# The weights' rings at one end of SBUF and the layers' tiles at the other

## The chip, the cores and the metric

One core of one Trainium2 chip runs the whole program. The metric is the device time of one execution in microseconds (us), as the median over several runs. A difference of about 0.2% (2 us) is what a measurement of this kernel can tell from none.

## The reference, cut to what matters

Three transformer layers work on 256 tokens of width 1024, in float32. Each has a mixer and a gated feed-forward block of inner width 2816:

```python
h = rms_norm(x, norm_mix_g[layer])
x = x + mixer(h, ...)                          # layer 0: sparse attention and pooling
h = rms_norm(x, norm_ffn_g[layer])             # layer 1: stick-breaking attention
x = x + (silu(h @ w1) * (h @ w3)) @ w2         # layer 2: retention and block attention, gated
```

Nearly all the arithmetic is products of the 256 tokens with weight matrices that are read once, 172.6 MB in all.

## The kernel before, in words

A float32 product is made of three float32r products: each operand is split into a high part (hi) and a rest (lo), and hi x hi, hi x lo and lo x hi are added up (`mm3`, L198 to L204; lo x lo is dropped). The stationary operand of a matmul is 128 x 128 of the transposed tokens, the moving operand 128 x 512 of a weight matrix. Each matmul has its own weight load (LDWEIGHTS), which runs while the matmul before it streams.

**The weights** come through `Stream` (L112 to L168). SP loads 1 MB at a time into one of 4 slots w_raw (8 KiB a partition each); ScalarE copies a piece of 1024 words to w_hi (L147), VectorE subtracts to get w_lo (L148); both have rings of 5 slots of 4 KiB a partition. `tick` (L296) keeps the loads and splits ahead of the matmuls.

**proj** (L315 to L347) makes 512 columns of a product over 8 blocks k of the width: for each piece (two k) six matmuls for the first 128 tokens into one accumulator, then six for the second 128 into another. Its stationaries are xT_hi and xT_lo, the normalized tokens. **outproj** (L353 to L397) makes all 1024 columns at once in four accumulators (128 tokens x 512 columns each): for each k and each half of the tokens it issues six matmuls at L368, on the two accumulators in turn. The last four k (the tail; two in the stick layer) are done accumulator by accumulator, 12 matmuls on each. Its stationaries are the layers' own tiles: hT_hi and hT_lo in the three feed-forward blocks (264 x 3 matmuls), mixT in the sparse layer, qT (reused for the attention's result) in the stick layer, moT, A0 and A1, B and C in the second layer.

Attention, transposes and norms are generators that `tick` steps between the matmuls. Line 832 in the stick layer multiplies parts of the constants cst_r (stationary) with sk_sh and sk_sl (moving, 384 columns); lines 1039 to 1041 in the retention multiply ret_sh and ret_sl (stationary) with A (moving, 256 columns).

**Where tiles lie.** Pools opened in `__init__` (L171 to L186) stay open to the end; each layer opens pools of its own and closes them, and the next layer's take the same bytes. All are laid from the low end of a partition's SBUF upwards in the order of opening. Bytes in a partition:

| tiles | before |
|---|---|
| const pool: ident, gains, cst_r (17,280) and others | 16,512 to 21,384 |
| w_raw | 21,408 to 54,176 |
| w_hi, w_lo | 54,176 to 74,656, 74,656 to 95,136 |
| x | 95,136 to 103,328 |
| xT_hi, xT_lo | 103,328 to 111,520, 111,520 to 119,712 |
| junk and the small pool | 119,712 to 124,448 |
| layers' pools | 124,448 to at most 222,752 |
| of these hT_hi, hT_lo | 124,448 to 146,976 to 169,504 |
| mixT | 173,632 to 190,016 |
| qT in the stick layer | 124,448 to 140,832 |
| sk_sh, sk_sl | from 197,152 |
| moT, B, C, A0 and A1 | 124,448, 132,640, 140,832, 157,216 to 181,792 |
| ret_sh | from 216,608 |

Counted modulo 512, the slots of w_hi and w_lo and xT_hi and xT_lo all start at 416; hT, the stick layer's qT, moT, A, B, C, sk_sh and ret_sh at 32; mixT at 64; the part of cst_r that L832 loads at 384. Steps inside a tile, from one stationary to the next or one moving piece to the next, are multiples of 512 bytes here.

Of the kernel before, what the change touches and what calls it, by code (L numbers as in the profile page):

```python
# [37 lines left out]
AHEAD = 4  # L38
# [73 lines left out]
class Stream:  # L112


    def __init__(self, nc, raw, hi, lo, ahead_load, ahead_split):
        self.nc, self.raw_p, self.hi_p, self.lo_p = nc, raw, hi, lo
        self.al, self.asp = ahead_load, ahead_split
        self.slots, self.pieces = [], []
        self.raws, self.parts = {}, {}
        self.i = self.loaded = self.split = 0  # L120
# [50 lines left out]
class Kernel:  # L171
    def __init__(self, ctx, tc, a, out):
        self.tc, self.nc, self.a, self.out = tc, tc.nc, a, out
        pool = lambda name, bufs, **kw: ctx.enter_context(tc.tile_pool(name=name, bufs=bufs, **kw))
        self.cp = pool("const", 1)
        self.raw = pool("raw", 4)
        self.hi = pool("whi", AHEAD + 1)
        self.lo = pool("wlo", AHEAD + 1)
        self.act = pool("act", 1)
        self.small = pool("small", 4)  # L180
        self.acc = pool("acc", 4, space=bass.MemoryType.PSUM)
        self.z = pool("z", 2, space=bass.MemoryType.PSUM)
        self.misc = pool("misc", 2, space=bass.MemoryType.PSUM)
        self.now = self.seq = 0
        self.late = slice(P, T)
        self.tasks = []  # L186
# [968 lines left out]
```

## Time and profile before

| what | value |
|---|---|
| median of 3 runs | 1026.62 us (1026.05 to 1026.72) |
| the profiled execution | 1026.29 us |
| its span, first to last instruction | 1024.2 us |
| TensorE (PE) busy | 1007.5 us, 4790 matmuls |
| weight loads (PEld) busy | 827.8 us |
| VectorE (DVE) busy | 631.1 us |
| ScalarE (ACT) busy | 548.5 us |
| HBM read | 172.60 MB, 170 GB/s over the span |

PE is the matmuls, PEld the weight loads, SPq SyncE's DMA queue. Matmuls are pipelined: one is recorded for longer than the distance to the next, so busy time doesn't tell how fast TensorE goes. The distance from one matmul's start to the next one's does. In the view of the chain in order of time, a piece "x220" is 220 matmuls one behind the other, with the time that they took together.

### The profile page before, as it was taken

What the parts mean: (1) busy time and instruction counts of PE and PEld (TensorE: products, weight loads), DVE (VectorE), ACT (ScalarE), POOL (GpSimd) and SP (SyncE); (2) the same over time, 40 slices, a digit from 0 to 9 for tenths busy, and PEclk for the clock granted to TensorE, in tenths of its full rate; (3) what the DMA queues carried; (4) which work ended last, traced back from release to release, by engine and by line L of the source; (5) the groups of instructions that cost most, each with busy time, mean ns of one, the idle gap of its engine ahead of it and who ended that gap; (6) DMA issues with size and microseconds to landing.
All of it is one profiled execution on the core that took longest, in us unless ns stands there. A gap on an engine that the chain in (4) does not pass through costs nothing.

```text
span 1024.2 us, 12484 instructions
## 1 busy us (share of the span) xinstructions
PE 1007.5 (98%) x4790; PEld 827.8 (81%) x4790; DVE 631.1 (62%) x896; ACT 548.5 (54%) x822; POOL 71.2 (7%) x171
## 2 busy tenths in 40 slices
PE   7999999999999999999999999999999999999998
PEld 6777888888778888788888888888887888888886
DVE  5987655554466888655554467666777665555542
ACT  7566544443467776744444366675444464444431
POOL 2321000000040000200000024000020010000000
PEclk9999999999999999999999999999999999999999
DMA  9443655555555333455555546455535546555531
GB/s 329 166 154 106 218 174 185 185 188 182 165 173 197 98 109 124 132 197 187 183 192 178 187 143 205 135 185 187 183 124 173 187 137 233 174 199 174 193 135 41
DMA packets 80747, 174.45 MB, mean 170 GB/s; under 512 B 3120, under 2 KB 16048, under 8 KB 80688
## 3 DMA queue, kind: packets, MB, share of 16 engines
q1 hardware_dynamic: 80400, 173.57, 49.8%
q8 instruction: 37, 0.61, 0.2%
q14 instruction: 22, 0.18, 0.0%
q10 hardware_dynamic: 288, 0.09, 0.0%
HBM read 172.60 MB, written 1.05 MB: 170 GB/s over the span
## 4 chain that ended last, share of the span: by engine, by line
PE 90%; DVE 4%; POOL 2%; ACT 2%; issue 1%; DMA 1%; SPq 0%; DVEq 0%; ACTq 0%
PE acc L368 27%; PE acc L202 18%; PE acc L204 18%; PE acc L203 18%; PE misc L223 4%; DVE w_lo L148 1%; POOL is_y L232 1%; PE z L204 1%; PE misc L202 1%; PE misc L203 1%; PE z L202 1%; PE misc L204 1%; PE z L203 1%; DMA x<-in_x_dram 1%; DVE sc L729 0%
## 5 line engine op out<-in xcount | busy, mean ns | idle before, releaser
L148 DVE TENSOR_TENSOR w_lo<-w_raw,w_hi 128x1024 fp32r<-128x1024 f32 (+1 forms) x323 | 392.9, 1222 | 298.4 <-ACT w_hi L147 298.1
L147 ACT CAST w_hi<-w_raw 128x1024 fp32r<-128x1024 f32 (+1 forms) x323 | 337.4, 1050 | 350.9 <-PE acc L204 225.9
L202 PE MATMUL acc<-w_hi,xT_hi 128*128 128x512 f32 (+2 forms) x896 | 352.8, 394 | 0.0
L204 PE MATMUL acc<-w_hi,xT_lo 128*128 128x512 f32 (+2 forms) x896 | 347.7, 388 | 0.0
L203 PE MATMUL acc<-w_lo,xT_hi 128*128 128x512 f32 (+2 forms) x896 | 347.7, 388 | 0.0
L204 PEld LDWEIGHTS acc<-w_hi,xT_lo 128*128 128x128 f32 x896 | 168.9, 188 | 34.8
L202 PEld LDWEIGHTS acc<-w_hi,xT_hi 128*128 128x128 f32 x896 | 169.0, 189 | 32.2 <-ACT xT_hi L213 1.0
L203 PEld LDWEIGHTS acc<-w_lo,xT_hi 128*128 128x128 f32 x896 | 169.2, 189 | 31.3
L368 PE MATMUL acc<-w_hi,hT_hi 128*128 128x512 f32 x264 | 105.1, 398 | 0.0
L368 PE MATMUL acc<-w_lo,hT_hi 128*128 128x512 f32 x264 | 104.1, 394 | 0.0
L368 PE MATMUL acc<-w_hi,hT_lo 128*128 128x512 f32 x264 | 86.9, 395 | 0.0
L368 PEld LDWEIGHTS acc<-w_hi,hT_hi 128*128 128x128 f32 x264 | 49.6, 188 | 12.5
L368 PEld LDWEIGHTS acc<-w_hi,hT_lo 128*128 128x128 f32 x264 | 49.6, 188 | 11.7
L368 PEld LDWEIGHTS acc<-w_lo,hT_hi 128*128 128x128 f32 x264 | 49.6, 188 | 10.9
L267 POOL TENSOR_TENSOR norm_s<-norm_ss 128x1 f32<-128x1 f32 x12 | 3.4, 282 | 597.6 <-ACT junk L263 597.6
L214 DVE SCALAR_TENSOR_TENSOR xT_lo<-misc,gains,xT_hi 128x128 fp32r<-128x128 f32 (+1 forms) x84 | 28.0, 353 | 21.1 <-ACT xT_hi L213 21.0
L213 ACT ACTIVATE xT_hi<-misc,gains 128x128 fp32r<-128x128 f32 (+1 forms) x84 | 29.0, 370 | 11.4 <-DVE xT_lo L214 9.5
L441 ACT ACTIVATE sg<-acc,norm_rstd 128x512 f32<-128x512 f32 (+1 forms) x36 | 23.6, 655 | 17.7 <-PE acc L204 17.0
L402 DVE TENSOR_TENSOR x<-acc,x 128x512 f32<-128x512 f32 x24 | 16.6, 690 | 14.2 <-PE acc L368 13.7
L446 DVE SCALAR_TENSOR_TENSOR hid<-acc,norm_rstd,sg 128x512 f32<-128x512 f32 (+1 forms) x36 | 23.9, 700 | 1.6 <-ACT sg L441 1.6
L263 ACT ACTIVATE junk<-x 128x512 f32<-128x512 f32 x24 | 15.2, 632 | 16.6 <-DVE x L402 14.7
L232 POOL TENSOR_TENSOR is_y<-is_v,mhalf 128x1 f32<-128x1 f32 (+2 forms) x24 | 23.8, 992 | 2.0
(265 smaller groups left out, 985.0 us busy)
## 6 DMA issues: line engine op xcount, KB each, us to landing
w_raw<-in_ffn_w_dram SPq DMA_DIRECT2D x62, 1024.0 KB, 5.0
w_raw<-in_w_in_dram SPq DMA_DIRECT2D x26, 1024.0 KB, 4.9
w_raw<-in_w_ffn_down_dram SPq DMA_DIRECT2D x11, 1024.0 KB, 5.0
w_raw<-in_w_ffn_gate_dram SPq DMA_DIRECT2D x10, 1024.0 KB, 5.0
w_raw<-in_w_ffn_up_dram SPq DMA_DIRECT2D x10, 1024.0 KB, 5.0
w_raw<-in_od_w_qkv_dram SPq DMA_DIRECT2D x8, 1024.0 KB, 5.1
w_raw<-in_ev_w_in_dram SPq DMA_DIRECT2D x5, 1024.0 KB, 6.5
w_raw<-in_ev_w_out_dram SPq DMA_DIRECT2D x4, 1024.0 KB, 6.4
```

The lines of the kernel that those rows point to most:

```text
L147: nc.scalar.copy(hi, raw)
L148: nc.vector.tensor_sub(lo, raw, hi.bitcast(F32))
L202: nc.tensor.matmul(out, ah, bh, start=start, stop=False, skip_group_check=True)
L203: nc.tensor.matmul(out, ah, bl, start=False, stop=False, skip_group_check=True)
L204: nc.tensor.matmul(out, al, bh, start=False, stop=stop, skip_group_check=True)
L213: nc.scalar.mul(hi, src, scale)
L214: nc.vector.scalar_tensor_tensor(lo, src, scale, hi.bitcast(F32), op0=OP.mult, op1=OP.subtract)
L223: self.nc.tensor.transpose(out, in_, self.ident)
L232: nc.gpsimd.tensor_tensor(y, v, self.mhalf[:, :width], op=OP.pow)
L368: mm = lambda a, b, start, stop: self.nc.tensor.matmul(o, a, b, start=start, stop=stop, skip_group_check=True)
L441: nc.scalar.activation(s[:, :m], acc[:, :m], AF.Silu, scale=n["rstd"][:, h:h + 1])
L446: nc.vector.scalar_tensor_tensor(t[:, :m], acc[:, :m], n["rstd"][:, h:h + 1], sg[h][:, :m], op0=OP.mult, op1=OP.mult)
```

## The change

The three pools of the weights' rings are opened on the right side: they are laid from the high end of SBUF downwards, and so end at byte 229,344, from 155,616 on. Everything opened after them on the left side (x, xT, the small pool, the layers' pools) moves down by the size of the rings, 73,728 bytes, which is a multiple of 512: x starts at 21,408, xT_hi at 29,600, the layers' pools at 50,720. The const pool stays. Modulo 512 the rings start at 480 and all others where they did.

```diff
         self.cp = pool("const", 1)
-        self.raw = pool("raw", 4)
-        self.hi = pool("whi", AHEAD + 1)
-        self.lo = pool("wlo", AHEAD + 1)
+
+        self.raw = pool("raw", 4, side="right")
+        self.hi = pool("whi", AHEAD + 1, side="right")
+        self.lo = pool("wlo", AHEAD + 1, side="right")
         self.act = pool("act", 1)
```

## Rows read from the trace of the kernel before

**Rows 1.** The page, busy time by engine, and the granted clock in 40 slices

```profile
PE 1007.5 (98%) x4790; PEld 827.8 (81%) x4790; DVE 631.1 (62%) x896; ACT 548.5 (54%) x822; POOL 71.2 (7%) x171
...
PEclk9999999999999999999999999999999999999999
```

**Rows 2.** The page, the chain that ended last, by engine and by line

```profile
PE 90%; DVE 4%; POOL 2%; ACT 2%; issue 1%; DMA 1%; SPq 0%; DVEq 0%; ACTq 0%
PE acc L368 27%; PE acc L202 18%; PE acc L204 18%; PE acc L203 18%; PE misc L223 4%; DVE w_lo L148 1%; POOL is_y L232 1%; PE z L204 1%; PE misc L202 1%; PE misc L203 1%; PE z L202 1%; PE misc L204 1%; PE z L203 1%; DMA x<-in_x_dram 1%; DVE sc L729 0%
```

**Rows 3.** Who waited for whom, and SP's queue: us in total, times, longest

```profile
ACT w_hi L147 <- PE acc L204: 225.9, 153, 3.8
...
PEld misc L223 <- DMA x<-in_x_dram: 6.0, 3, 4.1
...
SPq L136 <- DVE w_lo L148: 751.9, 135, 17.8
```

**Rows 4.** Timeline, proj, ten matmuls: start us, us, engine, line, tiles

```profile
139.74 0.39 PE L202 MATMUL acc<-w_hi,xT_hi 128*128 128x512 f32 x1
...
141.78 0.39 PE L202 MATMUL acc<-w_hi,xT_hi 128*128 128x512 f32 x1
```

**Rows 5.** The chain in order of time, pieces of outproj: start us, us

```profile
225.28 51.34 PE acc L368 x220
...
961.50 58.81 PE acc L368 x252
```

**Rows 6.** Windows: us, busy of PE, PEld, DVE, ACT, POOL; clock, DMA share, GB/s

```profile
127.00:144.00 17.00, 17.00 (x76) 14.08 (x76) 9.49 (x10) 7.59 (x8) 0.00 (x0) 1.00 0.55 178
...
1010.00:1019.00 9.00, 9.00 (x41) 7.22 (x40) 2.08 (x3) 0.00 (x0) 0.00 (x0) 1.00 0.16 58
```

**Rows 7.** Timeline, the last outproj's tail, nine matmuls

```profile
1009.40 0.40 PE L368 MATMUL acc<-w_hi,hT_lo 128*128 128x512 f32 x1
...
1011.27 0.40 PE L368 MATMUL acc<-w_lo,hT_hi 128*128 128x512 f32 x1
```

**Rows 8.** Timeline, proj after an interruption by transposes

```profile
37.50 0.39 PE L204 MATMUL acc<-w_hi,xT_lo 128*128 128x512 f32 x1
...
38.66 0.39 PE L203 MATMUL acc<-w_lo,xT_hi 128*128 128x512 f32 x1
...
39.79 0.39 PE L202 MATMUL acc<-w_hi,xT_hi 128*128 128x512 f32 x1
```

**Rows 9.** Groups by line and shape: busy us, mean ns, idle before

```profile
L148 DVE TENSOR_TENSOR w_lo<-w_raw,w_hi 128x1024 fp32r<-128x1024 f32 x320 | 389.7, 1224 | 296.9 <-ACT w_hi L147 296.5
L202 PE MATMUL acc<-w_hi,xT_hi 128*128 128x512 f32 x864 | 342.5, 396 | 0.0
```

**Rows 10.** Window over the whole span, line 368 alone: PE, PEld

```profile
0.00:1024.20 1024.20, 297.56 (x1224) 226.48 (x1224) 1.00 0.50 170
```

**Rows 11.** Timeline, the stick layer's line 832 and what follows

```profile
350.98 0.34 PE L832 MATMUL z<-sk_sh,cst_r 128*128 128x384 f32 x1
351.15 0.34 PE L832 MATMUL z<-sk_sl,cst_r 128*128 128x384 f32 x1
351.33 0.22 PE L834 MATMUL z<-sk_sh,cst_r 128*128 128x128 f32 x1
```

**Rows 12.** Timeline, 256 columns: ten matmuls of proj, six of the retention

```profile
27.05 0.28 PE L202 MATMUL acc<-w_hi,xT_hi 128*128 128x256 f32 x1
...
28.13 0.28 PE L202 MATMUL acc<-w_hi,xT_hi 128*128 128x256 f32 x1
...
753.15 0.28 PE L202 MATMUL misc<-A,ret_sh 128*128 128x256 f32 x1
...
753.75 0.28 PE L204 MATMUL misc<-A,ret_sl 128*128 128x256 f32 x1
```

**Rows 13.** Weight loads by line and shape: busy us, mean ns

```profile
L203 PEld LDWEIGHTS acc<-w_lo,xT_hi 128*128 128x128 f32 x896 | 169.2, 189 | 31.3
...
L202 PEld LDWEIGHTS misc<-A,ret_sh 128*128 128x128 f32 x12 | 2.3, 190 | 0.8 <-issue 0.7
```

## The prediction

> **What bounds the kernel now.** First the page's busy times and slices: TensorE is busy for 1007.5 us of the span of 1024.2 [rows 10], and the granted clock is full, 2.4 GHz, all the way [rows 1]. The profiled execution took 1026.29 us, 2.1 more than its span; the median of the runs is 1026.62, so sums against this execution come out 0.3 low. Second the chain that ended last: 90% of it is TensorE, over 80% the matmuls of proj (L202 to L204) and outproj (L368) on the accumulators [rows 2]. Third the waits: the copy that makes w_hi waits for TensorE to give ring tiles back (225.9 us behind proj's alone), and SP's loads wait 751.9 us for w_lo's maker to give raw slots back, so the stream of weights runs ahead; of TensorE's own waits the longest is 6.0 us, for x at the start [rows 3]. So the time is the number of matmuls times the gap from the start of one to the start of the next, and the gap is what to look at.
>
> There are two gaps for one shape (128x128 stationary, 512 columns, float32r). In proj nine gaps take 2.04 us: 226.7 ns each [rows 4]. In outproj the chain has 220 matmuls in 51.34 us and 252 in 58.81: 233.4 ns each [rows 5]. The granted clock is 1.00 in both [rows 6]. The slow gap is still there after 1010 us, where ScalarE does nothing, VectorE runs three instructions and the DMAs are at 0.16 [rows 6, 7], so it isn't other engines or loads that make it. After an interruption proj too is slow at first: the five gaps from 37.50 to 38.66 make 232 ns each, the next five, to 39.79, 226 [rows 8]. I call these the fast and the slow rhythm.
>
> **What the change does, part by part.** It issues no instruction more or less, moves none, adds no wait: pools are opened in the same order, so the layers' pools reuse each other's bytes as before, each 73,728 bytes lower. Only bytes change. Matmuls between two of the layers' tiles keep their distances. Four things could feel the rest.
>
> DMAs into w_raw: 170 GB/s on average, a busy share of 0.50, with the loads waiting for free slots [rows 3, 10]. Any small change is hidden by slots loaded ahead: 0 us.
>
> The splits: w_lo's subtraction, the longer of the two, takes 1,224 ns 320 times, 389.7 us in all and 296.9 idle before it, beside 1,007 of TensorE [rows 9]. It would have to slow by a factor before the rings of five ran dry; 0 us. What is not under TensorE on the chain (VectorE 4%, POOL 2%, ScalarE 2%, DMA 1%: some 92 us [rows 2]) I bound at 1% either way, 0.9 us, since no row shows such an instruction changing with the place of its tiles; I take 0.
>
> Outproj: 1,224 matmuls [rows 10]. All their stationaries (mixT, hT, qT, moT, A, B, C) lie at byte 124,448 or above; all of proj's (xT) end at 119,712. After the change every stationary of outproj ends below 116,300, so if height is what separates the rhythms, all 1,224 fall to 226.7. That is 6.7 x 1,224 = 8.2 us at most; the 192 of mixT and qT stand between pieces of attention, and after an interruption even xT's are slow for five gaps [rows 8], so I count them half: 6.7 x (1,032 + 96) = 7.5 us. The other end is 0; that they get slower still no steady row suggests, and the rivals' prices cover it.
>
> Proj: 864 x 3 = 2,592 matmuls of 512 columns [rows 9]. Below, kept rhythm: 0. Above, all of them in the slow rhythm: 6.7 x 2,592 = 17.4 us; some 288 of them (stick layer, six projections of 48) stand between attention's matmuls and mostly never settle, so 15.4. I take 0, for this reason. Byte distance is the second thing that separates the rhythms: counted modulo 512, xT starts 0 bytes from the ring tile that streams meanwhile, hT, qT, moT, A, B and C 128, mixT 160. After the change these are 448 (xT), 64 and 96 (mixT). The trace has one more distance: in the stick layer L832 loads parts of cst_r 352 bytes from the tile that streams, and its gaps are 170 and 180 ns for 384 columns [rows 11]. What should it be? Proj with 256 columns stands 120 ns apart and with 512 226.7, so a column costs 0.417 ns and a matmul 13.3 more [rows 4, 12]; 384 columns then make 173 in the fast rhythm, 180 in the slow. A mean of 175 is near the fast one. So 0 and 352 are fast or nearly, 128 and 160 slow; 448 lies between 352 and 512, which is 0 again, and I expect proj to stay fast. For outproj 64 lies halfway from fast to slow: by this reading the gain is about half, 3.8 us.
>
> Is it height or distance? The stationaries of L202 to L204 on ret_sh, at byte 216,608 and distance 0 from A, which streams, stand 120 ns apart at 256 columns, just as proj's at 256 columns do [rows 12]. That speaks against height. Weight loads take 189 ns from xT and 190 from ret_sh [rows 13], which speaks against it too. The distance would do, but rests on four values. Both readings give a gain, so the sum is **1026.3 - 7.5 = 1018.8; against the median 1019**, with 1022.8 for the half gain.
>
> The Trainium skill, "TensorE: Matmul & The Clock Gate", in "Step-by-step: what each phase is for", says that TensorE has two read ports of SBUF of its own, so that loading the next weights takes no bandwidth from the running matmul. By that rule no tile's place could change a gap and the sum would be 1026.3. The trace has two gaps for one shape [rows 4, 5], which the rule doesn't explain; the ports themselves no row shows.
>
> **The rivals.**
> *Same: the order of work makes the slow rhythm.* Outproj alternates two accumulators and takes a new ring tile for each k; proj stays on one accumulator and uses a tile for two k. Then nothing moves: 1026.3. Against it: in outproj's tail twelve matmuls run on one accumulator, as in proj, and are no faster (1009.40 to 1011.27: eight gaps, 234 ns) [rows 7]. For it: nothing else rules it out, and the two gaps may also hang on bytes that keep their distance to each other. This is also how the change would do nothing of what it says: 0.24.
>
> *Slower: proj loses its rhythm.* If distance 0 is a special case and any other gives the slow rhythm, 448 is slow too. Place: all proj's stretches; price 15.4 us: 1041.7. For it: the only steady fast gaps in the trace have distance 0 [rows 4, 12]; after interruptions proj itself runs at the slow gaps [rows 8], as if slow were the rule. Against it: L832. It decides as soon as proj loses more than 7.5 us / 2,592 = 2.9 ns a matmul. 0.25. With outproj at 64 fast all the same, 1034.2: 0.10.
>
> *Much faster: the matmul's fixed part goes.* 13.3 ns in proj, 20 in outproj: 2,592 x 13.3 + 1,224 x 20 = 59 us, 967. Against it: pairs of tiles at most 60 KB apart (proj) and 180 KB apart (L832) both show it [rows 4, 11]. 0.02.
>
> **How the numbers follow.** Outproj fast and proj fast, 1017 to 1021: 0.28. Half gain, around 1022.8: 0.11. Much faster 0.02. That is 0.41 for faster by over 0.2% (2 us, about what a measurement of this kernel can tell from no change); 0.24 for within; 0.25 + 0.10 = 0.35 for slower. Signs are mixed, so the likeliest case's own range is 1017 to 1021, and the range of all reaches from 1017 to 1042: it leaves out the much faster case, the upper half of the 15.4 us case and some of the edges, under 0.2.
>
> **What would show it.** Right: in the chain, outproj's long pieces at about 226.7 ns a matmul (220 in 49.9 us instead of 51.34), proj's nine gaps still 2.04 us, all counts of instructions unchanged, TensorE's clock at 1.00, the busy times of ScalarE and VectorE as now. Half right: outproj's pieces near 230. Wrong, same: 51.34 us again. Wrong, slower: nine gaps of proj at 2.10 us and the span at 1039. I would be wholly wrong if the instructions stood in another order, or if a wait for w_lo showed on TensorE.

## The result and the profile after

| | before | after |
|---|---|---|
| median of 5 runs | 1026.62 us (1026.05 to 1028.32) | 1031.82 us (1030.82 to 1034.97) |
| span of the profiled execution | 1024.2 us | 1029.7 us |
| TensorE busy, matmuls | 1007.5 us, 4790 | 1013.5 us, 4790 |

The ratio after to before is 1.0051, 95% interval 1.0036 to 1.0066: the changed kernel is **slower** by about half a per cent, where the forecast was 0.7% faster. In the changed kernel all line numbers from 176 on are higher by one: L202 to L204 are L203 to L205, L368 is L369.

The page of the kernel after (busy time and number of instructions by engine; the granted clock in 40 slices; the chain that ended last, by engine), against [rows 1, 2]:

```profile
PE 1013.5 (98%) x4790; PEld 829.0 (81%) x4790; DVE 631.0 (61%) x896; ACT 548.3 (53%) x822; POOL 71.3 (7%) x171
...
PEclk9999999999999999999999999999999999999999
...
PE 90%; DVE 4%; POOL 3%; issue 2%; ACT 1%; DMA 1%; SPq 0%; DVEq 0%; ACTq 0%; POOLq 0%
```

The same instructions, and VectorE, ScalarE and GpSimd as busy as they were; TensorE takes 6.0 us more. (A slice of the clock is 26 us long and its digit 9 says 90% or more, so the short dip told below doesn't show in it.) The splits and the loads didn't change either. The group of w_lo's subtraction by shape, against [rows 9]:

```profile
L148 DVE TENSOR_TENSOR w_lo<-w_raw,w_hi 128x1024 fp32r<-128x1024 f32 x320 | 389.5, 1223 | 302.2 <-ACT w_hi L147 301.7
```

And the waits of SP's queue and of the copies to w_hi (us in total, times, longest), against [rows 3]:

```profile
ACT w_hi L147 <- PE acc L205: 229.7, 153, 3.9
...
SPq L136 <- DVE w_lo L148: 757.6, 135, 17.8
```

One subtraction takes 1223 ns (1224 before), and the loads still wait over 750 us for free slots. So the stream is as far ahead as it was, and the place to look at is again the gap between matmuls.

**Outproj is unchanged.** The chain in order of time, the long pieces of outproj (start us, us), against [rows 5]:

```profile
225.90 51.36 PE acc L369 x220
...
547.75 51.36 PE acc L369 x220
...
966.99 58.84 PE acc L369 x252
```

51.36 and 58.84 us, where before had 51.34 and 58.81: 233.4 ns a matmul, the slow gap. None of the 7.5 us came.

**Proj is slower.** For this I take a longer stretch than [rows 4]: 72 gaps in one unbroken run of proj in the last feed-forward block. The timeline of before, the first and the last of its 73 matmuls:

```profile
841.48 0.39 PE L204 MATMUL acc<-w_hi,xT_lo 128*128 128x512 f32 x1
...
857.80 0.40 PE L204 MATMUL acc<-w_hi,xT_lo 128*128 128x512 f32 x1
```

And the timeline of after, the same 73 matmuls:

```profile
846.07 0.39 PE L205 MATMUL acc<-w_hi,xT_lo 128*128 128x512 f32 x1
...
862.55 0.40 PE L205 MATMUL acc<-w_hi,xT_lo 128*128 128x512 f32 x1
```

16.32 us before, 16.48 after: 226.67 against 228.89 ns a matmul. Over the three matmuls of one float32 product (hi x hi, hi x lo, lo x hi) that is 680.0 against 686.7 ns, so each triple has lost 6.67 ns, 16 steps of the 2.4 GHz clock. All 24 long runs of proj in the trace of after (more than 30 matmuls without a break) settle at this figure within 0.2 ns; I call it the settled gap. Proj has 864 triples, which would make 5.8 us if all were in such runs; matmul for matmul the two traces drift apart by 4.3 us from 30 us on, the dip told next left out, and 4.2 of them lie in proj. It is less than 5.8 since the gaps right after an interruption were slow before too [rows 8].

The spans differ by 5.5 us. The rest is one step of 1.6 us at the border of the first two layers, and a start that is 0.4 us shorter. Windows of after and then of before (us, busy of PE, PEld, DVE, ACT, POOL, granted clock, DMA share, GB/s):

```profile
286.00:299.00 13.00, 10.80 (x52) 8.61 (x51) 8.24 (x15) 8.91 (x18) 9.89 (x12) 1.00 0.59 206
299.00:302.40 3.40, 3.40 (x10) 2.62 (x9) 2.63 (x3) 1.53 (x3) 0.00 (x0) 0.50 0.41 142
```

```profile
286.00:299.00 13.00, 10.74 (x52) 8.63 (x51) 8.33 (x15) 8.63 (x19) 9.52 (x12) 1.00 0.67 228
299.00:302.40 3.40, 3.40 (x16) 2.77 (x16) 2.68 (x4) 2.23 (x3) 0.00 (x0) 1.00 0.26 73
```

In the profiled execution of after TensorE was granted half its clock (1.2 GHz) for 3.4 us: 10 matmuls instead of 16. Ahead of it the engine had stood idle for 2.2 us in 13, as long as in before, whose clock stayed at 1.00. Such a dip is in the profiled executions of six of the ten kernels below (faster ones and slower ones) and missing in the others. What decides it is open; I count it as 1.6 us that the execution had and that no run here puts down to a place of tiles.

### The profile page after: what moved, and what is told of

Its sections match the earlier page's. It is cut to its first block, busy times and chain, and to the rows that moved or that the text cites. A ratio compares the mean times of both kernels' runs of the same rounds, so it can differ in the third digit from the quotient of the medians.

```text
span 1029.7 us, 12484 instructions
## 1 busy us (share of the span) xinstructions
PE 1013.5 (98%) x4790; PEld 829.0 (81%) x4790; DVE 631.0 (61%) x896; ACT 548.3 (53%) x822; POOL 71.3 (7%) x171
## 4 chain that ended last, share of the span: by engine, by line
PE 90%; DVE 4%; POOL 3%; issue 2%; ACT 1%; DMA 1%; SPq 0%; DVEq 0%; ACTq 0%; POOLq 0%
PE acc L369 27%; PE acc L203 18%; PE acc L205 18%; PE acc L204 18%; PE misc L224 4%; POOL is_y L233 1%; PE z L205 1%; PE z L203 1%; DVE w_lo L148 1%; PE misc L204 1%; PE misc L203 1%; PE z L204 1%; PE misc L205 1%; POOL kT L880 1%; DMA x<-in_x_dram 1%
## 5 line engine op out<-in xcount | busy, mean ns | idle before, releaser
L203 PE MATMUL acc<-w_hi,xT_hi 128*128 128x512 f32 (+2 forms) x896 | 356.0, 398 | 0.0
L205 PE MATMUL acc<-w_hi,xT_lo 128*128 128x512 f32 (+2 forms) x896 | 349.8, 391 | 0.0
L204 PE MATMUL acc<-w_lo,xT_hi 128*128 128x512 f32 (+2 forms) x896 | 348.6, 389 | 0.0
L205 PEld LDWEIGHTS acc<-w_hi,xT_lo 128*128 128x128 f32 x896 | 169.2, 189 | 37.6
L204 PEld LDWEIGHTS acc<-w_lo,xT_hi 128*128 128x128 f32 x896 | 169.5, 189 | 32.8
L203 PEld LDWEIGHTS acc<-w_hi,xT_hi 128*128 128x128 f32 x896 | 169.4, 189 | 32.1 <-ACT xT_hi L214 0.9
L369 PE MATMUL acc<-w_hi,hT_hi 128*128 128x512 f32 x264 | 105.2, 398 | 0.0
L369 PE MATMUL acc<-w_lo,hT_hi 128*128 128x512 f32 x264 | 104.4, 396 | 0.0
L369 PE MATMUL acc<-w_hi,hT_lo 128*128 128x512 f32 x264 | 86.9, 395 | 0.0
L369 PEld LDWEIGHTS acc<-w_hi,hT_hi 128*128 128x128 f32 x264 | 49.6, 188 | 12.3
L369 PEld LDWEIGHTS acc<-w_hi,hT_lo 128*128 128x128 f32 x264 | 49.6, 188 | 11.8
L369 PEld LDWEIGHTS acc<-w_lo,hT_hi 128*128 128x128 f32 x264 | 49.6, 188 | 11.1
L214 ACT ACTIVATE xT_hi<-misc,gains 128x128 fp32r<-128x128 f32 (+1 forms) x84 | 29.2, 369 | 11.4 <-DVE xT_lo L215 9.1
```

Source lines behind the costliest of these rows:

```text
L203: nc.tensor.matmul(out, ah, bh, start=start, stop=False, skip_group_check=True)
L204: nc.tensor.matmul(out, ah, bl, start=False, stop=False, skip_group_check=True)
L205: nc.tensor.matmul(out, al, bh, start=False, stop=stop, skip_group_check=True)
L214: nc.scalar.mul(hi, src, scale)
L369: mm = lambda a, b, start, stop: self.nc.tensor.matmul(o, a, b, start=start, stop=stop, skip_group_check=True)
```

## The experiments

A distance is where a stationary tile starts minus where a ring tile starts, in bytes. After the change all distances modulo 512 are new (xT 448, most of outproj's stationaries 64), and the rings lie at another end. The first pair of runs parts these two.

In all diffs below `n` stands for a number of words added to a tile that is used no further than before; everything that is allocated after it moves up. "xT" stands for proj's stationaries, "hT" for outproj's. Times are medians; the kernel before ran on the same chip beside each.

**1. Rings at the far end, old distances.** The changed kernel with x longer by 64 bytes (n = 16): distances 0 (xT) and 128 (hT), as before the change.

```diff
-        self.x = act.tile([P, 2, D], F32, name="x")
+        self.x = act.tile([P, 2 * D + n], F32, name="x")[:, :2 * D].rearrange("p (h d) -> p h d", d=D)
```

> The changed kernel with x padded by 64 bytes: the rings stay at the far end, but xT again starts 0 bytes (modulo 512) from the ring tiles and hT, qT, moT, A, B, C 128, as in the kernel before. Theory 'distance' (a gap hangs on the distance modulo 512 of the stationary that is loaded from the tile that streams): proj back at 226.7 ns, outproj at 233.3, median 1026.6 (1025.5 to 1028). Rival 'place' (the far end itself costs proj its rhythm): proj at 229 ns as in the changed kernel, 1031 to 1032.

Measured: 1026.04 us (1025.11 to 1029.40, 12 runs), ratio to before 0.9991, interval 0.9982 to 1.0001. Timeline, the same 73 matmuls of proj, first and last:

```profile
843.99 0.39 PE L205 MATMUL acc<-w_hi,xT_lo 128*128 128x512 f32 x1
...
860.31 0.39 PE L205 MATMUL acc<-w_hi,xT_lo 128*128 128x512 f32 x1
```

16.32 us, the fast gap. The far end costs nothing that these runs can tell: the whole loss goes with the 64 bytes.

**2. Rings at the near end, new distances.** The kernel before with the same edit and n = 112 (448 bytes): distances 448 and 64.

> The kernel before, rings at the near end, with x padded by 448 bytes: distances as in the changed kernel (xT 448, hT and the like 64, mixT 96). 'Distance': proj at 229 ns, outproj at 233.3, 1031.5 to 1033. 'Place': proj at 226.7, 1026.6.

Measured: 1031.02 us (1029.99 to 1031.77, 5 runs), ratio 1.0034, interval 1.0022 to 1.0046. Timeline, the same 73 matmuls:

```profile
845.40 0.39 PE L204 MATMUL acc<-w_hi,xT_lo 128*128 128x512 f32 x1
...
861.88 0.39 PE L204 MATMUL acc<-w_hi,xT_lo 128*128 128x512 f32 x1
```

16.48 us, exactly the gap of after, with the rings where they always were, and a drift of 4.1 us from 30 us on, 3.9 of them in proj, with the clock at 1.00 all the way. The time is 0.5 us under the expected range; the gap is the expected one. So the two runs together show that the byte distance is the cause, and the end of SBUF is not.

**3. All at distance 0, rings near.** If the distance decides, outproj should become fast too when its stationaries are put at 0. The kernel before with junk longer by n = 96 words, and one small tile of the sparse layer (wis) made a whole 512 bytes, so that what follows it stays in step.

```diff
-        junk = self.act.tile([P, 512], F32, name="junk")
+        junk = self.act.tile([P, 512 + n], F32, name="junk")[:, :512]
...
-        wis = sp.tile([P, 2, 4], F32, name="wis")
+        wis = sp.tile([P, 128], F32, name="wis")[:, :8].rearrange("p (h j) -> p h j", j=4)
```

> The kernel before with the junk tile padded by 384 bytes and the small tile wis by 480, so that the stationaries of outproj (hT, qT, moT, A, B, C, mixT) too start 0 bytes modulo 512 from the ring tiles. 'Distance': outproj falls from 233.3 to 226.7 ns, 1224 x 6.7 = 8.2 us at most, 7.5 with the interrupted ones at half: median 1018.4 to 1019.5. Rival 'order of work' (outproj's slow gap comes from its alternating accumulators and tiles) and 'place': 233.3 as before, 1026.6.

Measured: 1022.75 us (1021.82 to 1023.11, 5 runs), ratio 0.9954, interval 0.9941 to 0.9967: faster than both kernels. The chain, outproj's long pieces:

```profile
225.60 49.90 PE acc L368 x220
...
544.40 49.90 PE acc L368 x220
...
959.01 57.17 PE acc L368 x252
```

226.8 and 226.9 ns a matmul where it was 233.4, with the same order of work. The direction and the gap came as expected, the gain is 3 to 4 us less than expected. Three things are in that by the trace: the three feed-forward blocks gave 4.7 us and not 5.3 (6.67 x 792), as some of their matmuls follow an interruption; the outprojs of the layers themselves, cut up by attention, gave 1.2 us of the 2.2 counted for them; and the clock dip, which the profiled execution of before lacks, took 1.6 back. A window of the kernel with all at 0 (columns as above):

```profile
296.60:300.00 3.40, 3.40 (x10) 2.62 (x9) 2.71 (x3) 1.64 (x3) 0.00 (x0) 0.50 0.60 209
```

The mean granted clock of each run tells how often this happens: it is 0.998 or less in every profiled execution with a dip, and 0.999 or 1.000 in the others. By it all 5 runs of this kernel had a dip, but only 4 of the 17 runs of the kernel before on the same chip. So the dip came more often in this kernel than in the one before, and a part of the gain is lost to that; why is open (on the chip of run 4 it was 3 of 5 against 6 of 9).

**4. All at distance 0, rings far.** The changed kernel with n = 16 on x, n = 96 on junk and the same wis.

> The changed kernel, rings at the far end, with x, junk and wis padded so that every stationary of proj and outproj starts at distance 0 from the ring tiles. Theory (the remainder decides and the end of SBUF costs nothing): the time of the kernel with the rings near and all at 0, 1022 to 1023.5 us, proj and outproj both at 226.7 ns. Rival (the two ends together cost something that shows only once the matmuls are fast): 1025 us or more, with one of the two gaps above 227.5.

Measured: 1022.89 us (1020.59 to 1023.62, 5 runs), ratio 0.9950, interval 0.9936 to 0.9965. Proj's 73 matmuls in the timeline:

```profile
839.83 0.39 PE L205 MATMUL acc<-w_hi,xT_lo 128*128 128x512 f32 x1
...
856.15 0.39 PE L205 MATMUL acc<-w_hi,xT_lo 128*128 128x512 f32 x1
```

16.32 us, and outproj's pieces are 49.91 us as well. So the change as it was made, with the remainders kept in step, is faster than before by as much as the kernel with the rings near: which end of SBUF the rings lie at makes no difference that these runs can tell. The two of its runs that show a mean clock of 0.999 and 1.000 took 1020.59 and 1021.89 us.

**5. Exchange.** The kernel before with n = 32 on x: proj at 128, outproj at 0 modulo 256.

> The kernel before with x padded by 128 bytes: distances (modulo 256, since 256 was as good as 0) are exchanged, proj at 128, outproj at 0 (mixT 32). 'Distance': proj at 232.4 to 233.4 ns, outproj at 226.7; some 2304 settled gaps of proj x 6.7 = +15.4, outproj -6.5 to -7.5: 1033 to 1037. If proj were held at 226.7 by its order of work: 1020 to 1023.

Measured: 1033.35 us (1032.34 to 1033.75, 4 runs), ratio 1.0055, interval 1.0038 to 1.0072. Timeline, a long run of 73 matmuls of proj in the first feed-forward block, and below it the chain's last piece of outproj:

```profile
106.30 0.39 PE L204 MATMUL acc<-w_hi,xT_lo 128*128 128x512 f32 x1
...
123.10 0.40 PE L204 MATMUL acc<-w_hi,xT_lo 128*128 128x512 f32 x1
```

```profile
970.53 57.18 PE acc L368 x252
```

Proj takes 16.80 us for the 72 gaps, 233.3 ns each; outproj takes 57.18, 226.9 each. The two products have changed places, so neither gap belongs to the order of work of one of them. The sizes are smaller than expected: by the trace proj lost 11.4 us (15.4 expected) and outproj gave 6.1 (6.5 to 7.5); a clock dip took 1.6.

**6. Is the period 512?** The kernel before with n = 64 on x: distances 256 (xT) and 384 (hT).

> A look at two more distances: the kernel before with x padded by 256 bytes, proj at distance 256, outproj at 384 (mixT 416). 'Distance', if the gap rises from 0 to about 128 and falls again towards 512: proj at about 231 to 233 ns, outproj at 227 to 231; 1033 to 1038 in all. 'Place' and 'order of work': 226.7 and 233.3, 1026.6.

Measured: 1027.22 us (one run), the kernel before beside it 1027.21. Timeline, the 73 matmuls:

```profile
842.43 0.39 PE L204 MATMUL acc<-w_hi,xT_lo 128*128 128x512 f32 x1
...
858.75 0.40 PE L204 MATMUL acc<-w_hi,xT_lo 128*128 128x512 f32 x1
```

16.32 us: 256 does what 0 does (and 384 what 128 did: outproj's pieces are 51.34 and 58.81 again). The expectation of 1033 to 1038 failed, since it took the period for 512. Alone, this run would look as "place" and "order of work" said; runs 1 to 5 have ruled these out, and run 5 has outproj fast at 256. So the remainder counts **modulo 256**, as far as the pairs 0 and 256, 128 and 384 show it, and I take the 448 of the change as 192.

**7. What lies between.** The kernel before with n = 56 on x and n = 48 on junk (distances 224 for xT, 32 for hT), and one with xT shifted by 16 bytes inside its tiles, as in the diff, and hT by 112 in the same way (distances 16 and 240).

```diff
-        n["hi"] = self.act.tile([P, KD, T], F32R, name="xT_hi")
+        n["hi"] = self.act.tile([P, KD * T + 128], F32R, name="xT_hi")[:, 4:4 + KD * T].rearrange("p (k t) -> p k t", t=T)
```

> A look at two more distances: proj at 224, outproj at 32 (mixT 64), by padding x by 224 bytes and junk by 192. Known so far, modulo 256: 0 226.7; 64, 96, 128 233.3; 192 228.9 ns. If the gap falls evenly from 128 to 256, 224 gives 227 to 228, if only 0 is special 229 to 233; 32 between 227 and 233. Time 1024 to 1032. A value below 226.7 would be new.

> Steps below 32 bytes: xT starts 16 bytes into its tiles (distance 16), hT 112 bytes into its own (distance 240), other layers' tiles at 128 as before. If the gap changes evenly with the distance: proj about 228, hT about 227 ns; if 16 and 240 count as 0: 226.7 both. Time 1021 to 1031.

Measured: 1039.99 us and 1029.44 us (one run each; before 1026.87). Timeline of the first (224), the 73 matmuls:

```profile
852.45 0.40 PE L204 MATMUL acc<-w_hi,xT_lo 128*128 128x512 f32 x1
...
869.25 0.40 PE L204 MATMUL acc<-w_hi,xT_lo 128*128 128x512 f32 x1
```

16.80 us: 32 bytes short of the fast place proj is as slow as at 128. An even fall would have given 227 to 228 ns; of the expected cases "only 0 is special" comes near, and the time lies outside the expected 1024 to 1032. 13.1 us were lost, about 1.5 of them to a clock dip as above; by the trace, matmul for matmul, proj lost 12.6 us, of the 15.4 that the rival in which proj loses its rhythm was priced at. The timeline of the second (16), a run in the first and the one in the last feed-forward block:

```profile
106.36 0.40 PE L204 MATMUL acc<-w_hi,xT_lo 128*128 128x512 f32 x1
...
123.16 0.39 PE L204 MATMUL acc<-w_hi,xT_lo 128*128 128x512 f32 x1
...
844.35 0.39 PE L204 MATMUL acc<-w_hi,xT_lo 128*128 128x512 f32 x1
...
860.67 0.39 PE L204 MATMUL acc<-w_hi,xT_lo 128*128 128x512 f32 x1
```

16.80 us and 16.32 us, for the same instructions on the same tiles. Of the 24 long runs of proj in this execution 15 go at 233.3 ns and 9 at 226.7, and none in between. So at 16 bytes the gap is not the 228 of an even change: it is one of two rhythms, and which one a stretch falls into changes from stretch to stretch.

**8. Which of the tiles must agree?** Two kernels in which one of proj's four tiles (xT_hi, xT_lo, w_hi, w_lo) is out of step. In the first xT_lo stands at 128 (outproj, as before, too; junk is longer by another 128 bytes for that); in the second w_lo's ring does, and all else, outproj's stationaries with it, is at 0 as in run 3.

```diff
-        n["hi"] = self.act.tile([P, KD, T], F32R, name="xT_hi")
+        n["hi"] = self.act.tile([P, KD * T + 32], F32R, name="xT_hi")[:, :KD * T].rearrange("p (k t) -> p k t", t=T)
```

```diff
-        lo = self.lo_p.tile([P, PIECE], F32R, name="w_lo")[:, :kc * n]
+        lo = self.lo_p.tile([P, PIECE + 128], F32R, name="w_lo")[:, 32:32 + kc * n]
```

> Which pair counts: xT_lo alone is moved to distance 128, xT_hi stays at 0 (outproj stays at 128). xT_lo is loaded while w_lo streams (the gap that starts at L203), and is then the stationary of the matmul in which w_hi streams (the gap that starts at L204). 'Load against stream': the gap of L203 grows by up to 20 ns, so that three gaps make 687 to 700 ns instead of 680. 'Own pair': the gap of L204 grows. If neither pair counts alone, all three gaps stay at 226.7. Time 1027 to 1034.

> Rings near, all stationaries and w_hi at distance 0, and w_lo's ring alone moved by 128 bytes. Of three matmuls of proj (L202 and L204 stream w_hi, L203 streams w_lo) only L203's stream stands off the stationary it uses and off the one that is loaded meanwhile. If the gap hangs on the tile that streams against the stationaries (in use or being loaded): only the gap that begins with L203 grows to 233, three gaps make 686.7 ns, and the time is 1022.75 + 6.7 x 864 + 6.7 x about 400 of outproj = 1031 us. If what counts is that two tiles with different remainders stream one behind the other: both gaps around L203 grow, three make 693 ns, and the time is about 1039 us.

Measured: 1035.81 us and 1034.23 us (one run each; before 1026.87 and 1027.72). The timeline of the first, the 73 matmuls:

```profile
849.41 0.40 PE L204 MATMUL acc<-w_hi,xT_lo 128*128 128x512 f32 x1
...
866.05 0.40 PE L204 MATMUL acc<-w_hi,xT_lo 128*128 128x512 f32 x1
```

And the timeline of the second, the 73 matmuls in the first and in the last feed-forward block:

```profile
105.38 0.40 PE L204 MATMUL acc<-w_hi,xT_lo 128*128 128x512 f32 x1
...
122.02 0.40 PE L204 MATMUL acc<-w_hi,xT_lo 128*128 128x512 f32 x1
...
847.49 0.39 PE L204 MATMUL acc<-w_hi,xT_lo 128*128 128x512 f32 x1
...
864.29 0.40 PE L204 MATMUL acc<-w_hi,xT_lo 128*128 128x512 f32 x1
```

16.64 us for the first, 693.3 ns a triple: by line (means of some 1,460 settled gaps of the trace) 226.7 behind L202, 232.5 behind L203, 234.2 behind L204. 16.64 and 16.80 us for the second, and there all three gaps are long, in the mean over both rhythms: 234.8, 233.2 and 230.6. A rule by pairs of tiles that are read at the same time doesn't fit the second kernel: while L204 streams w_hi, the stationary in use, the one that is loaded and the stream all stand at 0, and the gap still grows. Both expectations of that run fall, and each of the first one's alone does too: the gaps of L203 and of L204 both grew, and its time is 1.8 us over the range, with a clock dip of some 1.5 in it. What the two show is that one odd tile of four is enough to slow most of the triple. Through which pair it acts stays open.

The readings of outproj that are not shown yet, the chain's last piece of it in runs 1, 2, 4 and 6 and in the two kernels of run 7 (224 and 32, then 16 and 240), in this order:

```profile
963.94 58.59 PE acc L369 x252
...
966.24 58.81 PE acc L368 x252
...
959.77 57.18 PE acc L369 x252
...
962.45 58.81 PE acc L368 x252
...
975.22 58.81 PE acc L368 x252
...
965.89 57.57 PE acc L368 x252
```

**All distances together**, by the settled gap (proj: 72 gaps; outproj: the piece of 252):

| distance mod 256 | from | us | ns a matmul |
|---|---|---|---|
| 0 | proj before, runs 1, 3, 4, 6 | 16.32 | 226.7 |
| 0 | outproj, runs 3 to 5 | 57.17 to 57.18 | 226.9 |
| 16 | proj, run 7 | 16.80 or 16.32 | 233.3 or 226.7 |
| 32 | outproj, run 7 | 58.81 | 233.4 |
| 64 | outproj after, run 2 | 58.84, 58.81 | 233.4 |
| 128 | proj, run 5; outproj before | 16.80; 58.81 | 233.3 |
| 192 (as 448) | proj after, run 2 | 16.48 | 228.9 |
| 224 | proj, run 7 | 16.80 | 233.3 |
| 240 | outproj, run 7 | 57.57 | 228.5 |

In run 5 half of the long stretches of proj (12 of 24) go at 232.4, in run 1 outproj has a piece of 58.59 (232.5) at 128. All settled stretches of proj at 226.7, 228.9, 231.1 (run 8) and 233.3 are 102, 103, 104 and 105 times 6.67 ns for a triple, in the mean over a stretch: in the first stretches of run 5 single triples alternate between 704 and 696 ns. Proj's 232.4 isn't such a number.

## Why the prediction was wrong, point by point

*What bounds the kernel* was right: the time followed the gap between matmuls in every run. Beside it only the clock dips (1.6 us each) and the start of the program (up to some 1.2 us) moved.

*DMAs and splits at 0, the work outside TensorE at 0* held: 1223 ns a subtraction against 1224, loads waiting 757.6 us against 751.9, the chain's shares the same within a point.

*Outproj: 7.5 us* failed, both as height and as "64 lies halfway from fast to slow". Outproj's pieces took 51.36 us, no gain at all. That height is not the cause was in the prediction's own rows (ret_sh [rows 12] and the loads [rows 13]), and I let the forecast keep the sum of the case that those rows spoke against. Runs 1 and 4 settle it: moving everything by 73,728 bytes does nothing where the remainders are kept.

*Proj: 0, because 448 lies between 352 and 512* is **the step that failed** and made the sign wrong. It has two faults. The period is 256 (run 6), so 448 and 352 are 192 and 96, and the slow 160 lies between them: by the prediction's own reading 448 then stands between a slow place and a fast one, not between two fast ones. And a gap can't be interpolated at all: run 7 shows that 16 bytes already give the slow rhythm in 15 of 24 long stretches, and 224, nearer to the fast place than 192, is slower than 192. L832's pair of 170 and 180 ns [rows 11], which I averaged to 175 and called near the fast one, was two gaps among others of its kind and no settled rhythm.

*The rival "proj loses its rhythm"* had the right place and, in "distance 0 is a special case", the right reason. Its price of 15.4 us assumed that all three gaps of a triple go to 233.3; at 192 a triple loses one step of 6.67 ns instead of three, and 4.3 us were lost by the trace. At 224 (run 7), where it loses all three, 12.6 us went, so the price was high even there. It was to decide from 2.9 ns a matmul on, set against 7.5 us gained in outproj; with nothing gained there, 2.2 ns were enough.

*The rival "order of work"* falls with runs 3 and 5: outproj runs at 226.9 in its own order, and proj at 233.3 in its own. I had given it 0.24, mostly for want of a reason against it.

*The range* of 1017 to 1042 holds 1031.8. It does so by the rival's reach, not by a case that gives this value: that is luck.

*The Trainium skill's rule* ("TensorE: Matmul & The Clock Gate", "Step-by-step: what each phase is for") of two read ports, one for the weights and one for the stream, would have given no change, as the prediction reads it. Bytes alone moved the time by 0.5% up (run 5) and by 0.5% down (runs 3 and 4), so the place of the stationary beside that of the stream does act on the gap here. Whether it is ports that collide, or banks, or something else, no run tells.

## What to carry to other kernels

Where float32r matmuls of 512 columns follow each other without a break, look at the remainder modulo 256 of the bytes at which the stationary tiles and the moving ones start, and pad so that all agree: here this was worth 0.5% against the tuned kernel, and having it wrong in the most frequent product cost over 1% (12.6 us by the trace at 224 in run 7, one execution). Any edit that moves a pool, be it for another reason, can change these remainders: compare them before and after, for the two ends of SBUF need not have the same one (416 and 480 here). And read a rhythm on a long unbroken run of matmuls (over 72 gaps, starts given to 10 ns tell 0.2 ns a matmul), not on a pair of them; where a gap takes only a few values, don't interpolate between them.

## What the runs showed of the hardware that was not expected

- The settled gap of a float32r matmul of 512 columns in proj takes few values: a triple is 680.0, 686.7, 693.3 or 700.0 ns in the mean over a stretch, steps of 6.67 ns, which are 16 of the 2.4 GHz clock. The exception is 697 ns (232.4 a matmul) in half of the long stretches of run 5. Only distance 0 modulo 256 always gave the lowest.
- The same code on the same tiles can settle in either of two of them (xT at 16 bytes: 9 long runs at 226.7, 15 at 233.3 in one execution), so a stretch locks into a rhythm and keeps it until it is interrupted.
- 192 (measured as 448, 64 bytes from the fast place) is faster than 224 (32 bytes from it): 228.9 against 233.3 ns, so the gap doesn't grow evenly with the way from 0.
- One tile of four out of step (w_lo alone, run 8) also lengthens the gap from L204 to L202, two matmuls that don't use it: 230.6 ns in the mean against 226.7.
- At the border of two layers, where TensorE stands idle for some 2 us in 13, the granted clock fell to 0.50 for 3.4 us in some profiled executions and not in others; each dip cost about 1.6 us of the 1020 to 1040. Run 1's execution had a second dip, at 24.8 us.
